# Second attention of a two-layer diffusion backbone: order of key copies, steps of key chunks, and keys moved in ten transfers

## The chip, the cores and the metric

The kernel runs on one core of a Trainium2 chip. The metric is the device time of one execution in microseconds (us); the profile is one further execution with the hardware profiler on. TensorE is called PE, VectorE DVE, ScalarE ACT, GpSimd POOL and SyncE SP.

## The reference, cut to what matters

Two layers run over 2048 latent tokens behind 256 context tokens. Layer 0 is windowed attention. Layer 1, which the change touches, is latent attention: all 2048 queries of 16 heads read all 2304 keys, which come, like the values, from one shared 128-wide latent by an up-projection.

```python
kv = (rmsnorm(ckv, kv_norm_g) @ w_ukv).reshape(bsz, S, B_HEADS, B_NOPE + B_V)
kn, v = kv[..., :B_NOPE], kv[..., B_NOPE:]
...
s = (jnp.einsum('bqhd,bkhd->bhqk', qn_b, kn_all)
     + jnp.einsum('bqhr,bkr->bhqk', qr_b, kr_all)).astype(jnp.float32) * scale
p = jax.nn.softmax(s, axis=-1).astype(dt)
return jnp.einsum('bhqk,bkhd->bqhd', p, v_all)
...
y = (o * jax.nn.silu(g)) @ w_o
```

## The kernel before, in words

Everything is computed in pairs of a rounded part (H) and what is left of it (L), so a product of two numbers takes three matmuls. The second attention is a loop of 256 steps, `step(n)` (L1305): one unit per step, 16 heads `h` of 16 blocks `b` of 128 queries each. Inside the loop the order of instructions on PE, ACT, DVE, POOL and SP is the order of the program (L1396), and a step works on several units at once, each at another stage:

- Unit n is scored (`score`, L1068): five key chunks (`KCH`, four of 512 keys and one of 256), three matmuls each (L1083 to L1085), into the PSUM tiles pA and pS; DVE takes them out and finds the maximum (L1090), and `maximum` (L1093) ends with m.
- Unit n - 1 gets its exponential on ACT (`expo`, L1105), and `halves` (L1107) splits the last 1536 of its 2304 probabilities into two 16-bit halves, hl: ACT casts (L1112), POOL subtracts (L1114), and SP issues a DMA transpose of each half into pT (L1113, L1115). There are two hl tiles in turn, so a cast waits until the transposes of two units ago have read theirs.
- Unit n - 2 has its other 768 probabilities transposed on PE (`turn`, L1124), cast by ACT and subtracted by DVE (`turned`, L1127, the subtraction one step later).
- Unit n - 4 is multiplied with the values (`value`, L1147, 18 matmuls in three groups), and later units are gathered (L1160), shifted, joined, normed and stored. `norms` (L1186) runs in steps whose b is 1, 5, 9 or 13: two PE transposes into the PSUM bank pR (L1194) and a DVE product that reads it (L1195). `store` (L1204) issues one DMA per four blocks on ACT's queue, in steps with b = 3, 7, 11 and 15; its outermost dimension is 2. Queries are loaded on that queue at b = 0, 4, 8, 12, gates at b = 1, 5, 9, 13.

Keys are made while other heads run. In a step of an odd head h below 15, `gen_k` (L1007) fills pR (`rbank`, L1039, one bank, which the norms use too) with one chunk of keys for heads h + 1 and h + 2 together (L1012 to L1014). Four operations take it out in the next step, through the list `todo`, there called `left`: ACT copies the keys of h + 1 (L1018) and DVE subtracts (L1019) straight into `kT[0]`; then ACT and DVE do the same for h + 2 into `stash`. `move_k` (L1022) brings the stash, 64 partitions of 2304 numbers for H and as much for L, to `kT[1]` by DMA on ACT's queue, during head h + 1. Values are made in the same way, one tile per step, in heads 2, 6 and 10 and in two steps of heads 3, 7 and 11 (`gen_v`, L1027, two operations in `left`).

Of the kernel before, what the change touches and what calls it, by code (L numbers as in the profile page):

```python
# [32 lines left out]
def body(ctx: ExitStack, tc: tile.TileContext, x, c, ctxt, c_ctx, norm_g_0, ada_w_0, ada_b_0,  # L33
# [3 lines left out]
    V, A, G, PE = nc.vector, nc.scalar, nc.gpsimd, nc.tensor  # L37

    def dma(out, in_, eng=None):
        f = [a.bitcast(F32) if a.dtype == F32R else a for a in (out, in_)]  # L40
        (eng or nc.sync).dma_start(out=f[0], in_=f[1])
# [453 lines left out]
    def load_gate(u):  # L495
        kv, t = u["kv"], u["t"]
        u["gt"] = late2_2.tile([128, 2, 128], F32, name="gt", tag="gt", bufs=2)
        dma(out=u["gt"], in_=ga_d[t // 3][:, 2 * kv:2 * kv + 2, (t % 3) * 128:(t % 3 + 1) * 128])
# [182 lines left out]
    for n in range(NE, nu + 3):  # L681
        if n == nu - 8:
            raw_3 = pre_2.tile([128, 4096], F32, name="wraw", tag="pre")
            wb_raw = raw_3[:, 0:KT * 416].rearrange("p (k n) -> p k n", n=416)
            for i in range(2):
                dma(out=wb_raw[:, 4 * i:4 * i + 4],
                    in_=b_w_in[i * 512:(i + 1) * 512, 0:416].rearrange("(k p) n -> p k n", p=128))
# [276 lines left out]
    KCH = [(i * 512, min(512, T - i * 512)) for i in range(5)]  # L964
# [8 lines left out]
    kT = [None, None]  # L973

    def key_tiles(pool, i):
        kT[i] = [pool.tile([96, T], F32R, name=f"kT{i}{j}", tag=f"kT{i}{j}") for j in range(2)]
        dma(out=kT[i][0][64:96, :], in_=krh_d)
        dma(out=kT[i][1][64:96, :], in_=krl_d)
# [3 lines left out]
    def wu_steps(j):  # L982

        st = {}

        def load():
            st["raw"] = wu_4.tile([128, 4, 2, 64], F32, name="wuraw", tag="wuraw", bufs=1)
            dma(out=st["raw"].rearrange("p h w d -> p (h w d)"), in_=b_w_ukv[:, j * 512:(j + 1) * 512])
            st["sb"] = wu_4.tile([128, 4, 64], F32, name="sb", tag="sb", bufs=1)
            dma(out=st["sb"].rearrange("p h d -> p (h d)"), in_=svb_d[j * 256:(j + 1) * 256].partition_broadcast(128))  # L990

        def scaled():
            G.tensor_tensor(out=st["raw"][:, :, 1, :], in0=st["raw"][:, :, 1, :], in1=st["sb"], op=ALU.mult)

        def part(w):
            if w == 0:
                st["H"] = wu_4.tile([128, 2, 4, 64], F32R, name="wuH", tag="wuH")
                st["L"] = wu_4.tile([128, 2, 4, 64], F32R, name="wuL", tag="wuL")
            split_w(st["raw"][:, :, w, :], st["H"][:, w], st["L"][:, w])
            if w:  # L1000
                wu[j] = [[t[:, i].rearrange("p h d -> p (h d)") for t in (st["H"], st["L"])] for i in range(2)]

        return [load, scaled, lambda: part(0), lambda: part(1)]

    stash = k0p.tile([128, T], F32R, name="ks", tag="ks")

    def gen_k(h, i, p):  # L1007

        k0, kn = KCH[i]
        ks = slice(k0, k0 + kn)  # L1010
        wH, wL = [t[:, (h % 4) * 64:(h % 4) * 64 + 128] for t in wu[h // 4][0]]
        PE.matmul(p[:, 0:kn], wH, ckH[:, ks], start=True, stop=False)  # L1012
        PE.matmul(p[:, 0:kn], wH, ckL[:, ks], start=False, stop=False)
        PE.matmul(p[:, 0:kn], wL, ckH[:, ks], start=False, stop=True)  # L1014
        res = []
        for src, kH, kL in ((p[0:64, 0:kn], kT[0][0][0:64, ks], kT[0][1][0:64, ks]),
                            (p[64:128, 0:kn], stash[0:64, ks], stash[64:128, ks])):
            res.append(lambda src=src, kH=kH: A.copy(out=kH, in_=src))  # L1018
            res.append(lambda src=src, kH=kH, kL=kL: V.tensor_tensor(out=kL, in0=src, in1=kH.bitcast(F32), op=ALU.subtract))  # L1019
        return res  # L1020

    def move_k(i):  # L1022
        dma(out=kT[1][i][0:64, :], in_=stash[64 * i:64 * i + 64, :], eng=A)

    vts = {}

# [12 lines left out]
    def rbank():  # L1039
        return psr_4.tile([128, 512], F32, name="pR", tag="pR")  # L1040
# [12 lines left out]
    def load_q(h, ch):  # L1053
        qf = qs_[h, ch] = q_4.tile([96, 2, 256], F32, name="qf", tag="qf", bufs=1)
        for w in range(2):
            dma(out=qf[:, w, :], in_=qb_d[2 * ch + w][:, h, :], eng=A)

    def split_q(h, ch, w):
        if w == 0:
            qf = qs_[h, ch].rearrange("p w q -> p (w q)")  # L1060
            qH, qL = [q_4.tile([96, 512], F32R, name=n, tag=n) for n in ("qH", "qL")]
            G.tensor_scalar(out=qH, in0=qf, scalar1=1.0, scalar2=0.0, op0=ALU.mult, op1=ALU.add)
            qs_[h, ch] = (qH, qL, qf)
        else:
            qH, qL, qf = qs_[h, ch]
            G.tensor_tensor(out=qL, in0=qf, in1=qH.bitcast(F32), op=ALU.subtract)  # L1066
# [60 lines left out]
    def turned(u, w):  # L1127
        for r in range(2):
            ph, pl = [u["pT"][:, i, 3 * r:3 * r + 3] for i in range(2)]
            if w == 0:  # L1130
                A.copy(out=ph, in_=u["pt"][r])  # L1131
            else:
                V.tensor_tensor(out=pl, in0=u["pt"][r], in1=ph, op=ALU.subtract)  # L1133
# [63 lines left out]
    def gated(u):  # L1197
        h, b = u["h"], u["b"]
        if b % 4 != 3:
            return  # L1200
        g = outs[h, b // 4]
        G.tensor_tensor(out=g["gt"], in0=g["o"].rearrange("p x q -> p (x q)"), in1=g["gt"], op=ALU.mult)
# [24 lines left out]
    def wo_load(q):  # L1227
        wraw[q] = x_5.tile([128, 512], F32, name="woraw", tag="woraw")
        dma(out=wraw[q], in_=b_w_o[q // 2 * 128:q // 2 * 128 + 128, q % 2 * 512:q % 2 * 512 + 512])
# [11 lines left out]
    for w in range(2):  # L1241
        split_q(0, 0, w)
    key_tiles(k1p, 1)
    for i in range(2):
        move_k(i)

    box = {}
# [54 lines left out]
    def at(n):  # L1302
        return units[n] if 0 <= n < nu else None

    def step(n):  # L1305

        us, ue, ut, uv = at(n), at(n - 1), at(n - 2), at(n - LAG)
        ug, uj, ud = at(n - LAG - 1), at(n - LAG - 2), at(n - LAG - 3)

        def values(lo, hi):  # L1310
            for t in range(lo, hi) if uv else ():
                value(uv, t)

        h, b, nxt = -1, -1, None
        if us:
            h, b = us["h"], us["b"]
            nxt = at(n - b % 4 + 4)
            if b % 4 == 0 and nxt:
                load_q(nxt["h"], nxt["b"] // 4)
            if b % 4 == 1:  # L1320
                load_gate(h, b // 4)
            if h and h % 2 == 0 and b in (4, 9):
                move_k(b // 9)

        if h % 4 == 0 and h < 12 and b == 6:
            nextw.extend(wu_steps(h // 4 + 1))
        if nextw and b in (6, 9, 11, 13):
            nextw.pop(0)()
        wos = [[q for q in range(16) if q * 12 // 16 == b - d] if h == 15 else [] for d in range(4)]
        for q in wos[0]:  # L1330
            wo_load(q)
        for q in wos[3]:
            wo_split(q, 1)

        left = todo[:]
        todo.clear()
        if ud:
            gated(ud)
        if uj:
            join(uj)  # L1340
        if nxt and b % 4 >= 2:
            split_q(nxt["h"], nxt["b"] // 4, b % 4 - 2)
        if ue:
            expo(ue)
        if left:
            left[0]()
        if at(n - 3):
            turned(at(n - 3), 1)
        if ug:
            gather(ug)  # L1350
        if left:
            left[1]()
        for _ in range(min(4, len(tail))):
            tail.pop(0)()
        if us:
            score(us, 0)
            score(us, 1)
            score(us, 2)
        values(0, 4)
        if ue:  # L1360
            halves(ue)
        if left[2:]:
            left[2]()
            left[3]()
        if at(n - LAG - 4):
            store(at(n - LAG - 4))
        for _ in range(min(4, len(tail))):
            tail.pop(0)()
        if ut:
            turn(ut)  # L1370
            turned(ut, 0)
        if ug:
            shift(ug)
        for q in wos[2]:
            wo_split(q, 0)
        if us:
            score(us, 3)
        if uj:
            norms(uj)
        values(4, 8)  # L1380
        if us:
            score(us, 4)
            maximum(us)

        if h % 2 and h < 15 and b < 10 and b % 2 == 0:
            todo.extend(gen_k(h + 1, b // 2, rbank()))
        elif h % 4 == 2 and h < 12:
            todo.extend(gen_v(h // 4 + 1, b, rbank()))
        elif h % 4 == 3 and h < 12 and b in (11, 13):
            todo.extend(gen_v(h // 4 + 1, 16 + b // 13, rbank()))  # L1390
        values(8, NT)
        for _ in range(min(4, len(tail))):
            tail.pop(0)()

    todo, nextw = [], []
# [86 lines left out]
```

## Time and profile before

| | us |
|---|---|
| time, median of 3 executions | 3679.45 |
| lowest and highest | 3671.76, 3682.73 |
| profiled execution, whole time | 3676.76 |
| profiled execution, span of its instructions | 3674.9 |
| PE busy | 3325.6 (90%) |
| DVE busy | 2570.2 (70%) |
| ACT busy | 2070.9 (56%) |
| POOL busy | 1942.7 (53%) |

The span is what the rows below are measured in; the whole time has 1.9 us more around it. The second attention runs from about 1836 to 3480 in it. Busy time of an engine counts the time in which one of its instructions was running; register work and the issuing of DMAs are not counted.

### The profile page before, as it was taken

The numbers are of one execution on the slowest core, as the hardware profiler recorded it, in microseconds if no ns is written. First come the engines' busy times: TensorE is split into PE (matmuls) and PEld (weight loads), VectorE is DVE, ScalarE is ACT, GpSimd is POOL, SyncE is SP. The second block draws the span as 40 slices with busy tenths as digits, with TensorE's granted clock in tenths as the row PEclk, the third lists the DMA queues.
The fourth block names the chain that finished last, engine by engine and source line by source line (L and its number), as shares of the span: only waits on it lengthen the run. The fifth ranks groups of instructions, "written<-read, shape, count | busy, mean of one in ns | idle before, by whom it ended". The sixth has DMA issues, their size and how long they took to land. (4 is left out here: it accounts for less than half of the span.)

```text
span 3674.9 us, 58842 instructions
## 1 busy us (share of the span) xinstructions
PE 3325.6 (90%) x20044; PEld 2759.8 (75%) x20044; DVE 2570.2 (70%) x6964; ACT 2070.9 (56%) x3216; POOL 1942.7 (53%) x1403
## 2 busy tenths in 40 slices
PE   7869987878788888999999999999989999999999
PEld 5868987755555565899977777777767777787777
DVE  7544532399999998544388777777767777777755
ACT  6101301355555566544387777877867777777711
POOL 5432442266656665221166666766666666667722
PEclk8989998889889999999999999999999999999999
DMA  7344334489999999333388979898999988999943
GB/s 248 135 137 151 105 129 159 144 184 206 193 201 193 207 212 220 108 103 90 101 144 143 155 137 152 151 148 145 147 142 144 151 140 145 154 143 174 199 132 119
DMA packets 1386249, 568.75 MB, mean 155 GB/s; under 512 B 1167246, under 2 KB 1343294, under 8 KB 1384794
## 3 DMA queue, kind: packets, MB, share of 16 engines
q1 hardware_dynamic: 1308576, 501.76, 68.1%
q10 hardware_dynamic: 77372, 63.23, 7.7%
q8 instruction: 158, 2.59, 0.3%
q14 instruction: 143, 1.17, 0.1%
HBM read 180.18 MB, written 87.92 MB: 73 GB/s over the span
## 5 line engine op out<-in xcount | busy, mean ns | idle before, releaser
L1114 POOL TENSOR_TENSOR hl<-s,hl 128x1536 f16<-128x1536 f32 x256 | 797.9, 3117 | 556.1 <-ACT hl L1112 535.4
L1105 ACT ACTIVATE s<-s,m 128x2304 f32<-128x2304 f32 x256 | 569.3, 2224 | 290.6 <-DVE m L1096 271.6
L1147 PE MATMUL pV<-pT,vt 128*128 128x256 f16 x4608 | 640.4, 276 | 26.3 <-DVE ox L1160 26.2
L1147 PEld LDWEIGHTS <-vt 128*128 128x128 f16 x4608 | 396.2, 98 | 203.9 <-issue 121.6
L1090 DVE TENSOR_SCALAR_CACHE_REDUCE s<-pS 128x512 f32<-128x512 f32 (+1 forms) x768 | 455.8, 599 | 124.8 <-PE pS L1085 103.8
L559 POOL TENSOR_TENSOR hl<-s,hl 128x1280 f16<-128x1280 f32 (+2 forms) x144 | 349.4, 2444 | 157.5 <-ACT hl L558 155.3
L1112 ACT CAST hl<-s 128x1536 f16<-128x1536 f32 x256 | 376.9, 1472 | 70.5 <-DMA pT<-hl 57.7
L542 ACT ACTIVATE s<-s,nm 128x640 f32<-128x640 f32 (+2 forms) x288 | 221.5, 770 | 258.8 <-DVE nm L535 258.8
L1090 DVE TENSOR_SCALAR_CACHE_REDUCE s<-pA 128x1024 f32<-128x1024 f32 x256 | 311.7, 1218 | 66.7 <-PE pA L1085 61.8
L319 PE MATMUL pm<-hH,wH 128*128 128x384 f32 x864 | 305.7, 355 | 44.5 <-DVE rt L333 23.6
L1083 PE MATMUL pS<-kT,qH 96*128 96x512 f32 (+1 forms) x768 | 318.3, 414 | 6.5 <-DVE s L1090 5.1
L321 PE MATMUL pm<-hH,wL 128*128 128x384 f32 x864 | 301.7, 352 | 11.3 <-POOL wL L93 11.2
L320 PE MATMUL pm<-hL,wH 128*128 128x384 f32 x864 | 302.8, 353 | 0.6 <-DVE hL L273 0.6
L1133 DVE TENSOR_TENSOR pT<-pt,pT 128x384 f16<-128x384 f32 x512 | 261.6, 552 | 42.7 <-ACT pT L1131 40.8
L1084 PE MATMUL pS<-kT,qH 96*128 96x512 f32 (+1 forms) x768 | 275.1, 358 | 0.0
L1085 PE MATMUL pS<-kT,qL 96*128 96x512 f32 (+1 forms) x768 | 273.7, 356 | 0.0
L1083 PE MATMUL pA<-kT,qH 96*128 96x512 f32 x512 | 221.5, 433 | 0.0
L1131 ACT CAST pT<-pt 128x384 f16<-128x384 f32 x512 | 218.5, 478 | 0.9
L1124 PE MATMUL pt<-ident,s 128*128 128x128 f32 x1536 | 212.5, 275 | 0.0
L319 PEld LDWEIGHTS pm<-hH,wH 128*128 128x128 f32 x864 | 172.5, 200 | 50.3 <-DVE rt L333 22.6
L1085 PE MATMUL pA<-kT,qL 96*128 96x512 f32 x512 | 201.5, 393 | 1.6 <-POOL qL L1066 1.6
L1084 PE MATMUL pA<-kT,qH 96*128 96x512 f32 x512 | 200.9, 392 | 0.0
(320 smaller groups left out, 8551.6 us busy)
## 6 DMA issues: line engine op xcount, KB each, us to landing
wraw<-in_a_w_in_dram SPq DMA_DIRECT2D x80, 256.0 KB
q<-q2d ACTq DMA_DIRECT2D x72, 256.0 KB
xt<-in_x_dram SPq DMA_DIRECT2D x32, 512.0 KB
adw<-in_ada_w_dram SPq DMA_DIRECT2D x64, 256.0 KB
xt<-x1d SPq DMA_DIRECT2D x30, 512.0 KB
qf<-qbd ACTq DMA_DIRECT2D x128, 96.0 KB
q2d<-qH SPq DMA_DIRECT2D x48, 192.0 KB
q2d<-qL SPq DMA_DIRECT2D x48, 192.0 KB
```

The costliest lines, as they stand in the source:

```text
L319: PE.matmul(p[:, 0:384], wH[k][:, cs_], hH[:, k, :], start=(k == 0), stop=False)
L320: PE.matmul(p[:, 0:384], wH[k][:, cs_], hL[:, k, :], start=False, stop=False)
L321: PE.matmul(p[:, 0:384], wL[k][:, cs_], hH[:, k, :], start=False, stop=(k == KT - 1))
L559: G.tensor_tensor(out=h4[:, gs, 1], in0=u["sp", w][:, :, 0:nh], in1=h4[:, gs, 0], op=ALU.subtract)
L1083: PE.matmul(p, qH[:, bs], kH[:, ks], start=True, stop=False)
L1084: PE.matmul(p, qH[:, bs], kL[:, ks], start=False, stop=False)
L1085: PE.matmul(p, qL[:, bs], kH[:, ks], start=False, stop=True)
L1090: V.tensor_scalar(out=s[:, ks], in0=p, scalar1=1.0, scalar2=None, op0=ALU.mult, op1=ALU.max, accum_out=mx[:, i - 1:i])
L1105: A.activation(out=s, in_=s, func=AF.Exp, bias=u["m"], scale=SC, accum_out=sm[:, b % 4:b % 4 + 1])
L1112: A.copy(out=hl[:, 0], in_=s[:, NP0:T])
L1114: G.tensor_tensor(out=hl[:, 1], in0=s[:, NP0:T], in1=hl[:, 0], op=ALU.subtract)
L1147: PE.matmul(u["acc"], vts[h // 4, t][:, h % 4, :], u["pT"][:, :, t], start=(t == 0), stop=(t == NT - 1))
```

## The change

`left[0]`, ACT's copy of a chunk out of pR, is called ahead of `expo` and no longer behind it; `left[1]`, the subtraction that follows on DVE, is called ahead of `gather`. Key chunks are made in steps 1, 2, 5, 6 and 9 of an odd head and no longer in 0, 2, 4, 6 and 8. `move_k` moves one key chunk of H or L, ten calls for a head at b = 3 to 12, where it moved the whole H at b = 4 and the whole L at b = 9; before the loop it is called ten times instead of twice.

```diff
-    def move_k(i):
-        dma(out=kT[1][i][0:64, :], in_=stash[64 * i:64 * i + 64, :], eng=A)
+    def move_k(q):
+        i, ks = q % 2, slice(*[sum(KCH[q // 2][:j + 1]) for j in range(2)])
+        dma(out=kT[1][i][0:64, ks], in_=stash[64 * i:64 * i + 64, ks], eng=A)
...
-    for i in range(2):
+    for i in range(10):
         move_k(i)
...
-            if h and h % 2 == 0 and b in (4, 9):
-                move_k(b // 9)
+            if h and h % 2 == 0 and 3 <= b < 13:
+                move_k(b - 3)
...
+        if left:
+            left[0]()
         if ue:
             expo(ue)
-        if left:
-            left[0]()
         if at(n - 3):
             turned(at(n - 3), 1)
+        if left:
+            left[1]()
         if ug:
             gather(ug)
-        if left:
-            left[1]()
...
-        if h % 2 and h < 15 and b < 10 and b % 2 == 0:
-            todo.extend(gen_k(h + 1, b // 2, rbank()))
+        if h % 2 and h < 15 and b in (1, 2, 5, 6, 9):
+            todo.extend(gen_k(h + 1, (1, 2, 5, 6, 9).index(b), rbank()))
```

## Rows read from the trace of the kernel before

**Rows 1.** Busy time by head: stretch, length, busy (instructions) of each engine, PEclk, DMA.

```profile
core 0: us, PE busy (x) PEld busy (x) DVE busy (x) ACT busy (x) POOL busy (x), PEclk, DMA share, GB/s
...
2029.00:2133.30 104.30, 101.66 (x684) 82.51 (x681) 79.83 (x233) 79.05 (x104) 67.84 (x41) 1.00 0.90 152
...
2236.30:2337.00 100.70, 96.83 (x635) 78.43 (x633) 75.25 (x218) 75.80 (x88) 69.90 (x46) 0.97 0.99 160
2337.00:2438.50 101.50, 97.70 (x650) 78.38 (x648) 81.20 (x227) 80.85 (x98) 66.96 (x41) 1.00 0.86 143
2438.50:2544.60 106.10, 101.99 (x684) 82.51 (x681) 79.70 (x233) 78.94 (x104) 67.90 (x41) 1.00 0.88 149
...
2647.60:2758.90 111.30, 97.02 (x635) 78.04 (x633) 75.18 (x217) 75.67 (x88) 69.86 (x46) 0.95 1.03 145
...
2860.40:2966.20 105.80, 102.19 (x684) 82.48 (x681) 79.55 (x233) 78.77 (x104) 67.88 (x41) 1.00 0.99 150
...
3069.50:3169.30 99.80, 96.83 (x636) 78.60 (x634) 75.12 (x218) 75.81 (x89) 67.05 (x41) 0.97 0.97 157
...
3270.90:3371.30 100.40, 96.22 (x636) 78.33 (x634) 75.15 (x218) 75.84 (x89) 67.14 (x41) 0.97 0.99 157
```

**Rows 2.** The same table for steps 0, 3, 5, 9, 10 of head 5.

```profile
2337.01:2343.50 6.49, 6.49 (x45) 5.13 (x43) 5.37 (x16) 5.63 (x7) 3.79 (x2) 1.00 1.16 179
...
2357.51:2363.61 6.10, 6.02 (x42) 4.69 (x40) 4.59 (x11) 4.92 (x7) 5.07 (x4) 1.00 0.53 103
...
2370.15:2377.66 7.51, 6.19 (x45) 4.95 (x42) 5.67 (x16) 4.92 (x7) 6.18 (x6) 1.00 0.86 165
...
2396.42:2403.52 7.10, 6.15 (x45) 4.95 (x42) 5.39 (x17) 4.93 (x7) 5.61 (x4) 1.00 0.92 182
2403.52:2409.32 5.80, 5.80 (x43) 4.70 (x40) 4.60 (x14) 4.95 (x6) 3.29 (x4) 1.00 0.52 95
```

**Rows 3.** The same table: steps 6 and 9 of head 12, steps 2 and 6 of head 6.

```profile
3104.82:3116.66 11.84, 8.87 (x42) 6.66 (x40) 5.14 (x15) 7.63 (x10) 8.16 (x6) 0.71 0.95 164
...
3128.25:3134.26 6.01, 6.01 (x45) 5.04 (x42) 4.92 (x15) 4.54 (x5) 3.96 (x4) 1.00 1.06 215
...
2451.67:2457.84 6.17, 6.17 (x45) 5.05 (x43) 4.55 (x14) 4.74 (x8) 4.08 (x3) 1.00 0.67 126
...
2477.49:2486.60 9.11, 6.55 (x45) 5.05 (x43) 5.25 (x15) 7.57 (x11) 7.04 (x4) 1.00 0.86 170
```

**Rows 4.** Groups by line: shapes, count | busy us, mean ns | idle before, its releasers.

```profile
L1112 ACT CAST hl<-s 128x1536 f16<-128x1536 f32 x256 | 376.9, 1472 | 70.5 <-DMA pT<-hl 57.7 <-issue 2.0 <-POOL ou L1184 0.8
...
L1194 PE MATMUL pR<-ident,rb 128*128 128x128 f32 x128 | 25.3, 279 | 29.1 <-DVE ks L1019 26.0 <-POOL rb L1183 3.0
```

**Rows 5.** Lines L1018 (ns min/median/max; who waits) and L1105 (its waits): us, times.

```profile
L1018 ACT CAST kT<-pR x35: 347/563/569, 1935.6 to 3230.5; 64x512 fp32r<-64x512 f32 x28, 64x256 fp32r<-64x256 f32 x7
...
  DVE kT L1019: 49.3, 35
...
  DVE m L1096: 271.6, 215
```

**Rows 6.** Timeline of PE and DVE: start us, us, instruction, [idle before <-releaser].

```profile
2368.89 0.40 PE L1014 MATMUL pR<-ckH,wuL 128*128 128x512 f32 x1
...
2369.28 0.15 DVE L1096 TENSOR_SCALAR m<-m 128x1 f32<-128x1 f32 x1
...
2375.59 0.41 PE L1194 MATMUL pR<-ident,rb 128*128 128x128 f32 x2 [1.32 <-DVE ks L1019]
...
2093.49 0.39 PE L1030 MATMUL pR<-wuH,ckH 128*128 128x256 f32 x1 [0.39 <-DVE gt L1195]
```

**Rows 7.** DMA: move issues; queue q10 in 2260.2 to 2263.4; ACT in head 2.

```profile
L41 ACTq DMA_DIRECT2D kT<-ks x14: 512/614/1550, 2054.9 to 3329.4; - x14
...
q10 hardware_dynamic: 141, 0.13, 12.8%
...
2055.50 2.23 ACT L1105 ACTIVATE s<-s,m 128x2304 f32<-128x2304 f32 x1 [2.79 <-DVE pT L1133]
```

## Prediction

> **What bounds the kernel now.** I read the page first: TensorE (PE) is 90% busy, so only stretches in which PE pauses or is slowed can give time back. The second attention is a loop of 256 steps (16 heads of 16 query blocks), so I then cut it by head: a table of busy time per head, from the first score matmul of one head to that of the next [rows 1]. A head in which nothing disturbs PE should cost 93.7: that is head 12 (99.80) less what its one long step has over 5.80. An odd head that makes the next keys costs 101.5 with 97.7 of PE work [rows 1]; even heads that make no values cost 99.8 to 111.3, and their mean granted clock is 0.95 to 0.97 where the others have 1.00. So there are two losses, and I cut one head of each kind by step.
>
> In the odd head [rows 2] a plain step takes 5.80 and PE never pauses in it. A step that makes a key chunk takes 6.49. Steps 5 and 9, which also hold the norms of an earlier block, take 7.51 and 7.10, and PE is busy for 6.19 and 6.15 of them (step 1 repeats step 5). The reason is in the waits: the transposes of L1194 stood 26.0 us in all for DVE's last subtraction of a key chunk [rows 4], 1.32 at one of them [rows 6]. Both use the one PSUM bank pR, and a bank filled in step 4 is released only late in step 5, where the norms want it. That release is late because DVE's first subtraction waits for ACT's copy (49.3 us in 35 times [rows 5]), and the copy stands behind the 2.2 us exponential [rows 7] on ACT.
>
> In the even head [rows 3] one step takes 11.84 at a mean granted clock of 0.71: after PE had stood, part of it ran at the lower of the two levels, 1.2 GHz instead of 2.4. It is the second after the first key move is issued. ACT's half-cast L1112 stood 57.7 us in all for the DMA transposes [rows 4]; its two hl buffers are not free while the transposes of two steps ago still read them. The second move, at b = 9, costs head 12 nothing: the step 6.01 [rows 3] is that of every step with norms.
>
> **Part 1: keys move in ten parts.** Removed are the stalls of even heads. Undisturbed cost: 93.7 for heads 4, 8, 12 and 14; for 2, 6 and 10, which also make values, 103.15, which is head 6's 106.1 less what its long step of 9.11 has over the 6.17 of the like step before [rows 3]. Excess over these by rows 1: head 2 1.15, head 4 7.0, head 6 2.95, head 8 17.6, head 10 2.65, head 12 6.1, head 14 6.7, together 44.15. A little of it lies in steps away from the moves; I take **43**. Head 8's 10 us above its like is one cascade; other executions may have another or none, so this term is known to about ±8.
>
> What comes instead: parts of 128 KB (64 rows of 2 KB where now 64 rows of 9 KB) at steps 3 to 12. No row shows a part. From below: nothing, as for the whole move at b = 9 (a gain is excluded, since the removed stall is already counted whole). From above: the long step's 6.04 in proportion to bytes, 6.04 x 128 / 576 = 1.34, for the parts that follow a store of the gated output (steps 4, 8 and half a part at 12): 3.4 per head, 23 for seven heads. Why those: while the first move waits, the ACT queue moves 141 packets at 12.8% of 16 engines [rows 7], two engines' worth, and that is the store's slow tail; a part queues behind it on these engines. I take 0.5 per head, **3.5**, near the lower end, because ACT has time to spare: it idles 271.6 us in 215 times, 1.26 each, before its exponential [rows 5], and a delay that is shorter than that moves nothing else.
>
> The rule of the Trainium skill (DMA: Bandwidth & Descriptors, Why a DMA increments its semaphore by 16 and not by 1) is that a transfer uses the largest number of engines up to 16 that divides its slowest dimension. The store's slowest dimension is 2, so the trace's 12.8% agrees; a part keeps 64 rows and would still use all 16.
>
> On ACT's own queue each even head issues eight more DMAs, 0.61 each [rows 7]: 4.9 per head, 34 in all. They go out while ACT's engine works or waits for DVE's maximum (the 1.26 above), so I cost them at nothing; with that cover gone they cost the 34. Queued behind them are the exponential and, through it, the half-cast and SP's transposes. Before the loop ten parts stand where two moves stand: 8 x 0.61 = 4.9 at most on ACT while it serves the last value casts; I take **2**.
>
> **Part 2: key chunks in steps 1, 2, 5, 6, 9.** The norms of steps 1, 5 and 9 now stand ahead of the chunk in the same step, and no chunk is pending when they want the bank. The new wait is the other way: the chunk's matmuls need the norms' DVE product (L1195) to have read pR. The rows show just that for value tiles: 0.39 at L1030 [rows 6]. Behind it on PE are the ten last value matmuls. Steps 2 and 6 both finish one chunk and make another in the same bank. Today the bank comes free 5.44 into the step (2375.59 [rows 6] less the step's start, 2370.15 [rows 2]); the next chunk's matmuls would want it at about 4.9, an estimate from the 0.69 that they and the 1 us or so that ten value matmuls take before a step of 6.49 ends. With the copy earlier I take a wait of 0.2; as late as now it is 0.5.
>
> **Part 3: ACT's copy ahead of the exponential.** In step 4 the chunk's last matmul starts at 2368.89 and takes 0.40; the maximum is ready at 2369.43 [rows 6]. So the copy (0.56 [rows 5]) starts about when the exponential would have, and puts it back by up to 0.5. ACT has 1.26 of idle there, so it only shifts; who waits for the exponential (half-cast, POOL, transposes of the next step) has a step's time. In return DVE's 1.4 wait in each of 35 steps goes, and with it the 0.30 by which the step after (b = 3: 6.10 [rows 2]) is longer than 5.80. Value tiles get the same reordering, but in their steps PE already runs through (6.17 of 6.17 busy [rows 3]); I take nothing (0 to 5, some twelve waits of 0.39).
>
> Odd head after, by steps from rows 2: ten plain steps 58.0; steps 1 and 5: 6.01 + 0.69 + 0.39 = 7.09 each; steps 2 and 6: 6.49 + 0.2 = 6.69 each; step 9: 6.01 + 0.35 + 0.39 = 6.75 (the chunk is half as long); step 13: 6.01. Sum 98.3 against 101.5: 3.2, for seven heads **22.3**. Ends: with 0.5 in steps 2 and 6 and 0.30 kept after both, 2.0 each, 14; with no wait on the norms' product, 4.4 each, 31.
>
> **Sum.** 43 - 3.5 + 22.3 - 2 = 59.8 off the profiled execution's 3676.8 (its span of 3674.9 and 1.9 around it): 3617.0. That execution lies 2.7 under the median of 3679.45, from which the sum would give 3619.6; between the two I forecast 3618.
>
> **Rivals.** (a) *The stall spreads instead of shrinking.* DMA engines read 0.97 to 1.03 busy in heads 4, 8, 12 and 14 [rows 1], so ten parts may cost as much as one lump, each a little. Then part 1 gives nothing: 3676.8 - 22.3 + 2 = 3656. Against it: the second whole move is free. 13%.
> (b) *The wait changes its place.* PE stands for the chunk's bank in steps 1, 2, 5 and 6 as long as it stood for the norms, and the later exponential eats the rest: part 2 and 3 give nothing, 3676.8 - 43 + 3.5 + 2 = 3639. For it: one bank still serves both. 12%.
> (c) *Slower: ACT is held at its queue.* Once in head 2, behind a query load's issue, ACT stood 2.79 before its exponential [rows 7] instead of 1.26, and head 2's excess is 1.15. If each part held ACT past its 1.26 of idle by as much, 70 x 1.15 = 80, which is more than all gains: 3676.8 + 80 - 22.3 + 2 = 3736 with the stalls kept, 3676.8 + 80 - 43 - 22.3 + 2 = 3694 without. It decides from 0.9 per part. Against it: 14 moves have a median issue of 0.61 and one over 1.5 [rows 7]. 5%.
> The Trainium skill (DMA: Bandwidth & Descriptors, Bandwidth) speaks against the change: batch transfers to 1 MiB or more, each has a fixed cost of about 2 us (measured there on GpSimd's path). By it 56 more transfers in a row would add an estimated 112 us; beside other work they would add nothing, and no row here shows a part's own landing time.
>
> **How the numbers follow.** The forecast has 70%, (a) 13%, (b) 12%, (c) 5%. The forecast's own ends: gains of 51 + 31 with nothing lost, 3595; 35 + 14 less 23 and 5, 3656; I take most of it within 3603 to 3634. The range reaches up through (b) and halfway to (a): 3603 to 3648. A measurement of this kernel can tell about 0.3%, 11 us, from no change. Faster by more: 0.91; within: 0.05 (a and b together, or some of c); slower: 0.04.
>
> **What would show it.** Right: even heads 4, 8, 12 and 14 near 94 with a granted clock of 1.00 and ACT's wait for the transposes near 10 us in all; no wait of L1194 on DVE; waits of about 0.39 at L1012 on L1195, 21 of them; odd heads at 98 to 99. Wrong: waits on the transposes at steps 5, 9 and 13 of even heads (a); PE waiting at L1012 on the key subtraction for over 0.5 (b); part issues of over 1.2 on ACT's queue with late exponentials behind them (c).

## The result, and the profile after

| | before | after |
|---|---|---|
| median, us (4 executions each) | 3675.61 | 3614.82 |
| lowest to highest | 3668.30 to 3682.73 | 3610.37 to 3625.80 |
| profiled execution, its span | 3676.8, 3674.9 | 3625.8, 3623.9 |
| up to the first score of the loop | 1835.6 | 1840.0 |
| the loop (first score of head 0 to first score of the last block) | 1628.3 | 1564.3 |
| behind it | 211.0 | 219.7 |

The ratio is 0.9839, interval 0.9806 to 0.9872: 60.8 us less, where 61 were forecast against the median of before as it stood then (3679.45). Two executions, one of e3 (5316.7) and one of the kernel before beside e12 (6679.0), ran in a slow state and are left out of every median and ratio below. The profiled execution of after is the slowest of its four. Its loop is 64.0 shorter; it gives 4.4 back before the loop and 8.7 behind it (the heads 0 and 15 at the ends are +0.3). Neither stretch is the same from run to run, whatever the kernel: over all fourteen profiles of this document the first lasts 1831.6 to 1843.5 and the last 208.6 to 220.1. So below I compare the loop, cut as in [rows 1]. In the changed kernel the lines from 1024 on are numbered one higher.

The busy table of after by head, for heads 2, 4, 5, 8 and 12:

```profile
core 0: us, PE busy (x) PEld busy (x) DVE busy (x) ACT busy (x) POOL busy (x), PEclk, DMA share, GB/s
2030.70:2131.50 100.80, 100.11 (x683) 82.51 (x681) 80.43 (x232) 81.55 (x105) 67.71 (x41) 1.00 0.95 156
2231.20:2328.70 97.50, 94.17 (x635) 76.44 (x633) 75.16 (x217) 75.81 (x88) 69.84 (x46) 1.00 0.98 166
2328.70:2427.40 98.70, 98.19 (x651) 78.98 (x648) 80.62 (x228) 81.54 (x99) 67.18 (x41) 1.00 0.86 147
...
2627.95:2724.50 96.55, 94.26 (x635) 76.43 (x633) 75.19 (x217) 75.81 (x88) 69.85 (x46) 1.00 1.03 167
...
3023.80:3117.70 93.90, 93.79 (x634) 76.52 (x632) 75.03 (x217) 75.81 (x88) 67.02 (x41) 1.00 1.02 167
```

Against [rows 1]: the odd head 5 fell from 101.5 to 98.7, head 4 from 100.7 to 97.5, head 8 from 111.3 to 96.6, head 12 from 99.8 to 93.9, and the granted clock is 1.00 in all of them. Heads 4 and 8 are still 2.9 to 3.8 above 93.7. The value head 2 fell from 104.3 to 100.8, which is below the 103.15 that I had called undisturbed.

The same table by step: steps 1, 2 and 9 of head 5, steps 10 and 13 of head 4, step 2 of head 6:

```profile
2334.53:2341.67 7.14, 6.97 (x48) 5.52 (x45) 6.04 (x17) 5.37 (x7) 5.49 (x5) 1.00 1.00 196
2341.67:2348.40 6.73, 6.73 (x45) 5.18 (x43) 5.12 (x14) 6.08 (x9) 4.40 (x4) 1.00 0.70 118
...
2385.43:2392.22 6.79, 6.62 (x47) 5.44 (x45) 5.70 (x16) 5.37 (x7) 5.81 (x4) 1.00 0.98 184
2289.87:2297.04 7.17, 5.96 (x43) 4.70 (x40) 4.56 (x14) 6.83 (x9) 5.27 (x4) 1.00 0.85 183
2308.64:2317.14 8.50, 6.38 (x45) 4.96 (x42) 5.05 (x15) 7.30 (x11) 6.55 (x6) 1.00 0.87 167
2440.28:2446.45 6.17, 6.17 (x45) 5.05 (x43) 4.48 (x14) 5.08 (x8) 4.07 (x3) 1.00 0.63 115
```

The groups by line of after that answer to [rows 4]:

```profile
L1113 ACT CAST hl<-s 128x1536 f16<-128x1536 f32 x256 | 377.0, 1473 | 51.2 <-DMA pT<-hl 29.7 <-issue 6.0 <-POOL rb L1184 1.1
...
L1195 PE MATMUL pR<-ident,rb 128*128 128x128 f32 x128 | 24.7, 273 | 4.7 <-POOL rb L1184 4.7
```

From the view of after's L1196 (the norms' DVE product), one line of those who waited for it, us and times:

```profile
  PE pR L1012: 3.6, 21
```

The norms no longer wait for DVE (26.0 before). The new wait is there as foretold, in 21 steps, at 0.17 each and not 0.39. ACT's wait for the transposes fell from 57.7 to 29.7.

**Where the value steps got faster.** PE and DVE of the kernel before, step 11 of head 2, which starts at 2101.11:

```profile
2103.38 0.42 DVE L1037 TENSOR_TENSOR vt<-pR,vt 128x256 f16<-128x256 f32 x1 [1.32 <-ACT vt L1036]
...
2104.86 0.69 DVE L1090 TENSOR_SCALAR_CACHE_REDUCE s<-pS 128x512 f32<-128x512 f32 x1
...
2105.60 0.39 PE L1083 MATMUL pS<-kT,qH 96*128 96x256 f32 x1
```

The same step of after, which starts at 2100.19:

```profile
2101.92 1.23 DVE L1091 TENSOR_SCALAR_CACHE_REDUCE s<-pA 128x1024 f32<-128x1024 f32 x1 [0.47 <-PE pA L1086]
...
2103.07 0.69 DVE L1091 TENSOR_SCALAR_CACHE_REDUCE s<-pS 128x512 f32<-128x512 f32 x1
...
2104.49 0.36 PE L1084 MATMUL pS<-kT,qH 96*128 96x256 f32 x1
```

The busy figures of the two steps:

```profile
2101.11:2107.45 6.34, 6.34 (x46) 5.06 (x43) 4.84 (x15) 4.71 (x7) 4.82 (x4) 1.00 0.56 108
```

```profile
2100.19:2106.31 6.12, 6.12 (x45) 5.05 (x43) 4.92 (x15) 4.91 (x7) 4.79 (x4) 1.00 0.64 121
```

Before, DVE stood 1.32 for ACT's value copy and began to read the first pS tile 3.75 into the step. The last score chunk, which goes into a pS tile again, started 4.49 in, 0.05 after that reading ended (2104.86 + 0.69 = 2105.55). After, the reading begins 2.88 in and the last chunk starts 4.30 in: 0.19 earlier. The step is 6.12 instead of 6.34, although PE read as busy throughout both.

**What is left of the stalls.** POOL and ACT of after around the start of step 12 of head 4, which is at 2302.84, ahead of the long step 13:

```profile
2301.14 1.27 POOL L1067 TENSOR_TENSOR qL<-qf,qH 96x512 fp32r<-96x512 f32 x1
...
2302.45 3.42 ACTq L41 DMA_DIRECT2D qf<-qbd  x2
2305.90 0.51 ACTq L41 DMA_DIRECT2D kT<-ks  x1
2306.46 2.22 ACT L1106 ACTIVATE s<-s,m 128x2304 f32<-128x2304 f32 x1 [4.54 <-DVE s L1091]
```

Two query loads behind the store of the gated output took 3.42 to issue, a key part 0.51 more, and the exponential started 0.05 after that, 3.64 after its maximum was ready (2302.82; the view puts the 4.54 of idle time down to DVE). This is rival (c) once, in small, though the issue that held ACT is a query load's and not a part's; head 8 has it too (step 13: 7.76). Heads 4 and 8 are the two of the four in which POOL also splits the next weights in step 11, so it reads the one query buffer late (until 2302.41) and the loads go out late, 0.4 ahead of step 12 where heads 12 and 14 have 1.6. The second load took 3.07 and 2.29 there, 0.46 and 0.49 in heads 12 and 14. Without moves (e5) and with the store split (e7) it took at most 1.01. Whether the late start is what makes it slow is not shown.

### The profile page after: what moved, and what is told of

Its sections match the earlier page's. It is cut to its first block, busy times and chain, and to the rows that moved or that the text cites. A ratio compares the mean times of both kernels' runs of the same rounds, so it can differ in the third digit from the quotient of the medians.

```text
span 3623.9 us, 58845 instructions
## 1 busy us (share of the span) xinstructions
PE 3310.2 (91%) x20044; PEld 2756.0 (76%) x20044; DVE 2570.0 (71%) x6964; ACT 2083.4 (57%) x3216; POOL 1945.2 (54%) x1403
## 5 line engine op out<-in xcount | busy, mean ns | idle before, releaser
L1113 ACT CAST hl<-s 128x1536 f16<-128x1536 f32 x256 | 377.0, 1473 | 51.2 <-DMA pT<-hl 29.7
```

What stands on the lines that cost most here:

```text
L1113: A.copy(out=hl[:, 0], in_=s[:, NP0:T])
```

## The experiments

Sums from the profiles: odd = the seven odd heads 1 to 13, value = heads 2, 6 and 10, even = heads 4, 8, 12 and 14; T = ACT's wait for the transposes in the second attention; slow = transposing DMAs that held SP for over 3 us, of 512. Times are medians; "of before" is the ratio to the kernel before on the same chip, with its interval.

| kernel | time (before) | of before | odd | value | even | T | slow |
|---|---|---|---|---|---|---|---|
| before | 3675.6 | | 715.6 | 316.0 | 412.0 | 57.7 | 123 |
| after | 3614.8 (3675.6) | 0.9839, 0.9806 to 0.9872 | 694.2 | 302.4 | 382.7 | 29.7 | 75 |
| e1 parts | 3643.9 (3673.2) | 0.9921, 0.9900 to 0.9942 | 718.0 | 309.8 | 381.6 | 26.6 | 106 |
| e2 steps | 3665.4 (3673.2) | 0.9982, 0.9963 to 1.0001 | 704.0 | 315.4 | 412.9 | 57.3 | 95 |
| e3 order | 3658.3 (3673.2) | 0.9969, 0.9950 to 0.9989 | 702.7 | 318.7 | 405.3 | 62.1 | 92 |
| e4 steps and order | 3653.1 (3673.2) | 0.9949, 0.9929 to 0.9969 | 693.6 | 306.8 | 414.0 | 62.2 | 79 |
| e5 after, no moves | 3600.9 (3675.0) | 0.9807, 0.9782 to 0.9833 | 693.7 | 302.6 | 374.7 | 10.9 | 63 |
| e6 after, parts away | 3607.6 (3675.0) | 0.9819, 0.9800 to 0.9838 | 693.7 | 302.4 | 375.1 | 5.5 | 67 |
| e7 after, store split | 3609.1 (3675.0) | 0.9820, 0.9802 to 0.9838 | 693.7 | 302.5 | 374.7 | 0.8 | 6 |
| e8 before, whole later | 3639.9 (3675.0) | 0.9905, 0.9890 to 0.9921 | 719.6 | 309.2 | 378.4 | 17.8 | 109 |
| e9 before, store split | 3629.6 (3662.9) | 0.9904, 0.9870 to 0.9938 | 715.2 | 309.4 | 383.7 | 15.0 | 20 |
| e10 after, whole later | 3615.4 (3662.9) | 0.9857, 0.9816 to 0.9899 | 693.7 | 302.4 | 380.6 | 20.8 | 80 |
| e11 before, burst | 3700.3 (3662.9) | 1.0089, 1.0059 to 1.0119 | 716.8 | 343.5 | 403.6 | 21.3 | 96 |
| e12 after, store split, whole later | 3611.8 (3666.4) | 0.9858, 0.9841 to 0.9876 | 693.3 | 302.4 | 374.6 | 0 | 19 |

**Theory**: the parts end the long steps of the even heads, the new steps and the new order give the odd heads about 3 each. **Rivals**: one of the three does it all, or they need each other. First each alone.

**Parts alone**, on the kernel before, with `move_k` as in the change:

```diff
-    for i in range(2):
+    for i in range(10):
         move_k(i)
...
-            if h and h % 2 == 0 and b in (4, 9):
-                move_k(b // 9)
+            if h and h % 2 == 0 and 3 <= b < 13:
+                move_k(b - 3)
```

> The kernel before with the ten parts alone. Theory (the three parts of the change act on different steps and their gains add): the seven even heads lose their long steps, about 36 us, little of it comes back in the steps behind a store, odd heads stay at 101.5 and value steps at 6.33; time 3675 - 36 = 3639. Rival (the even heads only got better because reordered copies gave ACT more room for late transposes): long steps stay, under 15 us, 3660 or more.

Measured: -29.3. The even heads lost 30.4, the value heads 6.2; the odd heads rose by 2.4, nearly all of it in step 9 of head 11 (9.16 for 7.41), where the norms stood 1.8 for the bank.

**Steps alone**:

```diff
-        if h % 2 and h < 15 and b < 10 and b % 2 == 0:
-            todo.extend(gen_k(h + 1, b // 2, rbank()))
+        if h % 2 and h < 15 and b in (1, 2, 5, 6, 9):
+            todo.extend(gen_k(h + 1, (1, 2, 5, 6, 9).index(b), rbank()))
```

> The kernel before with key chunks in steps 1, 2, 5, 6, 9 alone. Theory: the wait of the norms for the bank goes (26 us), but with DVE's subtraction as late as before the chunks of steps 2 and 6 wait about 0.5 for the bank and the steps after keep about 0.3; 2 us per odd head, 14 in all, 3661; even heads unchanged. Rival (the gain of the odd heads is the order's alone, the steps only move the wait): odd heads at 101 or more, 3672 to 3678.

Measured: -7.8, which the time alone does not tell from no change (0.9963 to 1.0001), and 11.6 in the odd heads, 1.7 each, where 14 were expected. Steps 3 and 7 of head 5 are 6.38 and 6.39 there, where after has 5.77 and before 6.11: with ACT's copy still behind the exponential, the step after a chunk stays long, which is what the order takes away.

**Order alone**:

```diff
+        if left:
+            left[0]()
         if ue:
             expo(ue)
-        if left:
-            left[0]()
         if at(n - 3):
             turned(at(n - 3), 1)
+        if left:
+            left[1]()
         if ug:
             gather(ug)
-        if left:
-            left[1]()
```

> The kernel before with the copy ahead of the exponential and the subtraction ahead of the gather alone. Theory: value steps go from 6.33 to 6.13 and their wait for the norms' product from 0.39 to 0.17, 2.3 us in each of heads 2, 6, 10; in odd heads the steps after a chunk lose their 0.3 and the norms still wait for the bank, but about 1 us instead of 1.35: 1.5 each; together 17 us, 3658. Rival (the copy puts the exponential back and ACT pays): no gain, or slower.

Measured: -14.8; 12.9 in the odd heads, 1.8 each. The value steps fell to 6.13 and 6.77 with this edit alone, where e1 and e2 have 6.33 and 6.98. Their sum rose all the same: one step of head 10 waited 12.3 us for the transposes. In the odd heads parts 2 and 3 nearly add up: 11.6 + 12.9 = 24.5 against 22.0 together (e4).

**Steps and order, with whole moves**: the changed kernel with `move_k` as before, two moves ahead of the loop and `b in (4, 9)`.

> The changed kernel with whole moves at b = 4 and 9 again (and two before the loop). Theory: odd heads at 98.7 and value steps at 6.13 as in the changed kernel, long steps of 9 to 12 back at b = 6 of the even heads; 28 us below the kernel before, 3647. Rival (the transposes are now better placed, so a whole move no longer stalls): within 10 us of the changed kernel.

Measured: -20.0. The loop is 1597.5 here and 1595.3 in e1, 30.8 and 33.0 under before, together 63.8, and the whole change takes 64.0 off it. So the two halves add up in the loop, as far as one profile of each can say: the even heads of the four kernels with whole moves at 4 and 9 and the old store lie between 405.3 and 414.0. (The medians, -29.3 - 20.0 = -49.3 against -60.8, have the stretches outside it in them.)

Then the stalls themselves. **Theory**: the store's slow tail on two engines holds what is queued behind it, so the place of a move decides. **Rival**: the size of a move decides.

**No moves in the loop**: the two lines `if h and h % 2 == 0 and 3 <= b < 13` and `move_k(b - 3)` taken out of the changed kernel, which then leaves out bringing the keys of the odd heads from head 3 on to `kT[1]`.

> The changed kernel without any key move inside the loop: it leaves out moving the keys of odd heads from head 3 on into the second key tiles, so those heads score against head 1's keys; all other work stays. Theory (the ten parts still cost a little: in the trace after the change ACT waits 1.4 to 3.9 us for the transposes at step 8 of the even heads, and PE loses 0.3 to 1.4 at step 10 in four of them, 3.7 us in all; in heads 4 and 8 step 13 is 2.5 and 1.4 longer behind an issue of 3.4 us on ACT's queue): the heads 4, 8, 12, 14 come to 93.5 to 94.5, ACT's wait for the transposes falls from 29.7 to under 10, time 5 to 9 below the changed kernel, about 3607. Rival (the rest of those waits comes from the store and the query loads, not from the parts): the waits at step 8 stay, time within 2 of the changed kernel.

Measured: heads 4, 8, 12 and 14 are 93.7, 93.7, 93.7 and 93.6. The parts thus cost 382.7 - 374.7 = 8.0 in the even heads of after.

**Parts away from the stores**:

```diff
-            if h and h % 2 == 0 and 3 <= b < 13:
-                move_k(b - 3)
+            if h and h % 2 == 0 and b in (1, 2, 3, 5, 6, 7, 9, 10, 11, 13):
+                move_k((1, 2, 3, 5, 6, 7, 9, 10, 11, 13).index(b))
```

> The changed kernel with the ten parts in steps 1, 2, 3, 5, 6, 7, 9, 10, 11, 13: none is issued in a step that also issues a store of the gated output or the first query load. Theory (a part issued right behind the store queues behind its slow tail on two engines, and holds up the transposes two steps later): ACT's waits at step 8 of the even heads go, time 3 to 8 below the changed kernel, about 3610. Rival (the waits come from the total number of transfers in flight there, wherever the part stands): the waits move to steps 9 to 11, time within 2 of the changed kernel. Slower is possible if the part at step 13 meets the last query load: step 13 or 14 would then be longer in several even heads.

Measured: the 8.0 are gone (375.1), and ACT has no wait of over 1 us for the transposes any more. As many parts, as large, cost 0.4 when none follows a store. (Stores go out in steps 3, 7, 11 and 15, behind the move of their step. So what the new steps avoid is 4, 8 and 12, right behind a store and beside the query loads; parts at 3, 7 and 11 stay, against what is said above. The next run separates the store from the loads.)

**The store split**, in the changed kernel:

```diff
-        dma(out=ob_d[b // 4][r0:r0 + 64, h // 2, :].rearrange("d (w q) -> w d q", w=2), in_=g["gt"], eng=A)
+        for w in range(2):
+            dma(out=ob_d[b // 4][r0:r0 + 64, h // 2, 256 * w:256 * w + 256], in_=g["gt"][64 * w:64 * w + 64, :], eng=A)
```

> The changed kernel with the store of the gated output as two transfers of 64 rows each in place of one whose outer count is 2; the same bytes go to the same places. Theory (the store's slow tail on two engines is what the parts queue behind): the queue then moves the store's packets at well over the 12.8 % of 16 engines, ACT's waits for the transposes at step 8 go, time 3 to 10 below the changed kernel. Rival (its cost is the issue on ACT's queue): 64 more issues of about 0.5 to 0.6, the waits of the exponential grow, time 0 to 20 above the changed kernel.

Measured: the parts at their old places cost nothing either (374.7), and six transposing DMAs of 512 are slow instead of 75. Without any move in the loop (e5) there are still 63. So most of them are slow for the store and not for the keys. 64 more issues on ACT's queue cost nothing that shows.

**Whole moves at steps 6 and 10**, in the kernel before:

```diff
-            if h and h % 2 == 0 and b in (4, 9):
-                move_k(b // 9)
+            if h and h % 2 == 0 and b in (6, 10):
+                move_k(b // 10)
```

> The kernel before with its two whole moves at steps 6 and 10 in place of 4 and 9: nothing is made smaller, nothing else changed. Theory by place (the long step is the first move meeting the store's tail of step 4; the move at step 9, without a store in its step or the one before, costs nothing): the long steps at step 6 of the heads 4, 8, 12, 14 go, these heads come to 94 to 96, time near the kernel before with ten parts alone, 3644 (gain about 29), and the small size of the parts is not what helped. Rival by size (a transfer of 576 KB holds up the transposes wherever it starts): the long step moves to step 8, the even heads stay at 100 to 111, time within 8 of the kernel before.

Measured: -35.2, not told apart from the ten parts of e1 (0.9890 to 0.9921 against 0.9900 to 0.9942). The heads 4, 12 and 14 come to 93.6 to 94.1, head 8 to 97.0. The new steps are also without the query and gate loads that stand beside the moves at 4 and 9, so this run alone does not single out the store; e9 does. In head 13, in which no key is moved, step 5 took 10.44: behind the store of step 3 two transposing DMAs held SP for 3.51 and 3.61, ACT's cast and chunk copy came late, and the norms stood 2.7 for the bank. So under the old chunk steps a head can stall behind a store without any move. Head 4 of this kernel, against 100.70 at 0.97 in [rows 1]:

```profile
2233.86:2327.98 94.12, 93.88 (x636) 76.47 (x633) 75.28 (x217) 75.94 (x88) 69.97 (x46) 1.00 1.04 171
```

**The store split alone**, in the kernel before, with its whole moves at 4 and 9 (the edit is that of e7):

> The kernel before with the store of the gated output as two transfers of 64 rows; the key moves stay whole, at steps 4 and 9. Theory (the store's slow tail on two engines is the cause of the long step: it holds the transposing DMAs, and a whole move behind it only adds to that): the long steps at step 6 of the heads 4, 8, 12, 14 go without any change to the moves, these heads come to 94 to 97, the value heads to 103, ACT's wait for the transposes falls from 57.7 to under 15, time about 3640 (gain 30 to 37). Rival (the bytes of a whole move right behind the store hold the transposes, on however many engines the store runs): the even heads stay at 98 to 110, the gain is under 15. Second rival (its own issues on ACT's queue, 64 more of 0.48): the exponential waits longer and the odd heads grow past 102.3; gain under 25.

Measured: -33.3. Heads 4 and 8 of it:

```profile
2235.26:2328.94 93.68, 93.68 (x635) 76.53 (x633) 75.14 (x217) 75.95 (x88) 69.95 (x46) 1.00 1.02 171
2636.66:2739.34 102.68, 96.57 (x635) 78.32 (x633) 75.03 (x217) 75.83 (x88) 69.94 (x46) 0.97 1.00 156
```

Three of the four even heads are at 93.6 to 93.7 with the whole move where it was. Head 8 is not: there the transposes held ACT for 3.85 behind the first whole move and 7.45 behind the second. In the kernel before, too, the second move, at b = 9, was not free in head 8. SP and ACT there:

```profile
2706.88 10.82 SPq L1115 DMA_TRANSPOSE pT<-hl  x1
```

```profile
2725.91 1.47 ACT L1112 CAST hl<-s 128x1536 f16<-128x1536 f32 x1 [11.46 <-DMA pT<-hl]
```

Step 11 took 18.17 for it. In the four kernels with the old store and whole moves at 4 and 9 (before, e2, e3, e4), step 6 of the heads 4, 8, 12 and 14 is long 16 times out of 16 (8.03 to 15.33), step 11 six times (7.96 to 18.17). So the store explains nearly all of the first stall; what makes the second move stall in some heads is not shown.

SP's queue in the kernel before and in this one, from step 3 of head 4 on, which has the store:

```profile
2257.89 6.18 SPq L1113 DMA_TRANSPOSE pT<-hl  x1
2264.17 3.04 SPq L1115 DMA_TRANSPOSE pT<-hl  x1
```

```profile
2256.83 1.53 SPq L1113 DMA_TRANSPOSE pT<-hl  x1
2260.02 3.35 SPq L1115 DMA_TRANSPOSE pT<-hl  x1
```

```profile
q10 hardware_dynamic: 154, 0.40, 58.8%
```

The first transposing DMA beside the store holds SP for 1.53 instead of 6.18; in both kernels it is issued ahead of the move, by 0.94 here and 0.68 before. The last line is ACT's queue of this kernel in 2259.2 to 2262.4, 3.8 behind the store's issue, as the stretch of [rows 7] starts 3.7 behind its own: 0.40 MB in 3.2 us at 58.8% of 16 engines, where 0.13 MB moved at 12.8%. The rule of the Trainium skill on how many engines a transfer uses (DMA: Bandwidth & Descriptors, Why a DMA increments its semaphore by 16 and not by 1) agrees: with 64 rows outermost in place of 2 it allows 16.

**Whole moves in free steps, other parts kept**: the kernel of e4 with `b in (6, 10)` and `move_k(b // 10)`.

> The changed kernel with its other two parts kept and the keys again in whole moves, at steps 6 and 10, two before the loop. Theory by place: the even heads 4, 8, 12, 14 sum to 375 to 380 as with ten parts away from the stores (375.1), time 3604 to 3612, no slower than the changed kernel; ten parts are then not needed, and 56 more issues on ACT's queue had cost nothing measurable. Rival (small parts are needed once the rest of the loop is tighter): the even heads sum to over 390, time 3620 or more.

Measured: even heads 380.6, less than the ten parts of after (382.7); most of the rest is in head 8 again (98.3). The time is not told apart from after (0.9816 to 0.9899 against 0.9806 to 0.9872). It is 3 to 11 above what I had expected, on a chip that was 12 faster in the kernel before than that of e6.

**Parts in a burst**, in the kernel before, with `move_k` and its ten calls ahead of the loop as in the change:

```diff
-            if h and h % 2 == 0 and b in (4, 9):
-                move_k(b // 9)
+            if h and h % 2 == 0 and b in (4, 9):
+                for j in range(5):
+                    move_k(2 * j + b // 9)
```

> The kernel before with the keys in ten parts, but five of them issued one behind the other in step 4 and five in step 9: the same place as the whole moves, the small size of the parts. Theory by place (what is queued behind the store's tail decides, however it is cut): long steps at step 6 stay, the even heads 4, 8, 12, 14 sum to 400 or more, gain under 12. Rival by size (rows of 2 KB let the transposes' packets through where rows of 9 KB don't): the even heads come to 94 to 97 each, gain about 28 as with the parts spread over ten steps.

Measured: +37.3, the only kernel slower than before. The even heads are near what the theory by place says (403.6), but not by its mechanism: T is only 21.3, where before has 57.7 with whole moves in the same steps. ACT was held at its own queue instead, so this run does not decide between place and size. ACT and DVE of this kernel at step 4 of head 2, and its head 6:

```profile
2057.70 6.02 ACTq L41 DMA_DIRECT2D kT<-ks  x5
2063.76 2.21 ACT L1106 ACTIVATE s<-s,m 128x2304 f32<-128x2304 f32 x1 [6.60 <-issue]
...
2066.36 0.43 DVE L1038 TENSOR_TENSOR vt<-pR,vt 128x256 f16<-128x256 f32 x1 [6.21 <-ACT vt L1037]
```

```profile
2453.14:2571.61 118.47, 108.42 (x684) 86.65 (x681) 80.32 (x232) 79.05 (x104) 67.91 (x41) 0.93 0.78 133
```

Five issues took 6.02, 1.20 each, and the exponential stood 6.60. That is rival (c), beyond its 0.9 per part. The value heads lose most (343.5): under the old order ACT's value copy stands behind that exponential, DVE stood 6.21 for it, and PE then 4.9 for DVE's reading of pS.

**Store split and whole moves in free steps**: e10 with the edit of e7.

> The changed kernel with its other two parts kept, the store as two transfers of 64 rows, and the keys in whole moves at steps 6 and 10, two before the loop. Theory (the store on all 16 engines and moves in steps without a store are enough; the keys needn't be cut at all): the even heads 4, 8, 12, 14 sum to 375 to 378, as with no moves (374.7), the loop from head 1 to head 14 is as short as with the split store and ten parts (1463), time 3600 to 3610, 0 to 15 below the changed kernel. Rival (a whole move of rows of 9 KB still holds a transposing DMA now and then: head 8 alone had a step of 13.5 with the split store and whole moves at 4 and 9, and one of 8.3 with whole moves at 6 and 10): one or two long steps stay in head 8, even heads at 380 to 385, time 3610 to 3620.

Measured: 3611.8 where before has 3666.4 (0.9858, 0.9841 to 0.9876); odd 693.3, value 302.4, even 374.6. Heads 4 and 8:

```profile
2230.40:2324.03 93.63, 93.63 (x636) 76.55 (x633) 75.15 (x217) 75.98 (x88) 69.93 (x46) 1.00 0.99 171
2623.15:2716.84 93.69, 93.69 (x636) 76.55 (x633) 75.19 (x217) 75.95 (x88) 69.97 (x46) 1.00 0.99 171
```

PE never pauses in either. The loop is 1552.7, e7's 1552.9, e6's 1554.4, after's 1564.3. So three kernels have a loop shorter by 10 to 12 than the changed one, but in the time none of them is told apart from it: the stretches before and behind the loop differ by as much (e12: 1839.2 and 216.6; e7: 1839.5 and 208.6).

## Why the prediction was right, step by step

By the sums of the table, in the profiled executions; the two heads at the ends of the loop (0 and 15) moved by 0.3 together.

| term | forecast | measured |
|---|---|---|
| long steps of the even and value heads, net of what the parts cost | 39.5 | 35.9 |
| odd heads | 22.3 | 21.4 |
| value steps by the order | 0 (0 to 5) | 7.0 |
| before the loop | -2 | -4.4 |
| behind the loop | 0 | -8.7 |

(35.9: 412.0 - 382.7 = 29.3, and 316.0 - 309.4 = 6.6 with the value heads of e9, in which the stall is gone and the order is the old one. 7.0: 309.4 - 302.4.)

**Part 1.** The undisturbed 93.7 and 103.15 per head were exact: heads without a stall have 93.6 to 93.7 (e5, e7, e12) and 103.1 to 103.2 (e9). The mis-sized term is what the parts cost: 3.5 for seven heads, against 8.0 in the even heads. Of these, 3.7 are step 10 of heads 4, 8, 12 and 14, behind parts that follow a store, as I had argued, and 4.2 are step 13 of heads 4 and 8, ACT held at its queue, which I had priced at nothing. ACT's wait for the transposes was to come near 10 and is 29.7; with the parts away from the stores it is 5.5. The cause that I gave, the store's tail on two engines, is what e9 and e7 show. But I had it only as the price of a part, and the gain as that of small parts; e8, e9 and e12 show that small parts are not needed for it, and e11 that five of them at once are worse than a whole move. That the second whole move is free, which I held against rival (a), was read from head 12 alone: 12.4 of head 8's excess of 17.6 is its step 11, behind the second move.

**Part 2 and 3, odd heads.** Right to 0.1 in most steps: 7.14, 6.73, 6.79 for 7.09, 6.69, 6.75. In steps 1 and 5 two errors cancel: the wait is 0.17 and not 0.39, and PE is busy for 6.97 and not 6.70 (6.01 + 0.69).

**Part 3, value heads.** This step failed. I took nothing because PE reads 6.17 busy of 6.17 [rows 3]. e3 shows that the order alone takes 0.20 off each such step. The timelines above place it at the last score chunk, which stood for a pS tile that DVE read late; the busy figure, whose ends are modelled, covered it. The bound of 5 was also too low, since it counted only the waits that the view names (0.39 each).

**Issues on ACT's queue.** 56 more in the loop were costed at nothing. e6 has them all, and its loop stands 0.5 above that without moves (1554.4 against 1553.9): right, as long as they stand one to a step and not right behind a store. Before the loop, the six profiles with ten parts have a mean start of 1839.0, the eight with two 1835.8: 3.2, with a spread of 12 in the second group, which neither confirms the 2 nor excludes it.

**Rivals.** (a) is wrong: no head is above 100.8. (b) is wrong: PE's wait for the chunk's bank in steps 2 and 6 leaves them at 6.73. (c) is wrong for this kernel as a whole and right in two steps of it, by a query load's issue, and e11 shows its price. That the forecast came within 4 us of the median owes something to luck: the 7.0 of the value heads stand against 3.6 too little in part 1, 0.9 in the odd heads and 2.4 before the loop, and the 8.7 behind the loop belong to this one execution.

## What to carry to other kernels

Where small waiting transfers stall beside a large one, look first for what both are queued behind: here a store whose outermost count was 2, and either splitting it (e9) or moving the other transfers to steps that do not follow it (e8) gave about as much as cutting them into ten (e1); both together (e12) left no stall in the even heads. Spread issues on a compute engine's queue one to a step; five in a burst held ACT for 6.6 us (e11). Before a reordering is priced at nothing because an engine reads 100% busy, check in the timeline whether one of its instructions starts right when another engine has freed its buffer.

## What had not been expected of the hardware

- The same issue can take very different times. Key parts took 0.49 in the median (e6) and 0.86 in a burst (e11); the two query loads behind a store took 0.82 in head 12 of after and 3.42 in head 4. A transposing DMA (L1113) held SP for 1.47 in the median of the kernel before and for 6.18 beside the store on two engines, 1.53 in the like place with the store split (e9).
- DMA engines at 0.99 to 1.02 busy in a head are not by themselves a sign of a stall: head 4 has that share with every step at 5.80 or 6.01 (e12) as with the long step (0.99 [rows 1]).
- PE "busy" throughout a step hid 0.20 of waiting in each value step.
